# Token-major projections with 512 weight columns in one pass instead of 256 in each of two

## The chip, the cores and the metric

The kernel runs on one core of a Trainium2 chip. The metric is the device time of one execution, in microseconds; the times before and after are medians of several runs. Matmuls run on TensorE (PE in the profile, its weight loads PEld), elementwise work on VectorE (DVE) and ScalarE (ACT), transfers are issued from SyncE (SP) and GpSimd (POOL).

## The reference

Two layers of a hybrid block work on 512 latent tokens and 256 context tokens of 1024 features. In each layer the modulated, normalized tokens `h` are multiplied by one input matrix, whose columns feed three mixers and their gates:

```
glu, q, k, v, rq, rk, rv, rg, gates = split(h @ w_in[l] + b_in[l])
a   = conv_module(glu, ...)                       # depthwise convolution over 31 tokens
att = latent_attention(rope(rms(q)), rope(rms(k)), v, k_c, v_c)   # 8 query heads, 2 key heads
ret = bidir_retention(rq, rk, rv, ...)            # 8 heads, a mean and a norm taken per head
x   = x + g1 * ((sig(ga) * (a @ w_pa) + sig(gb) * (att @ w_pb) + sig(gc) * (ret @ w_pc)) @ w_out)
x   = x + g2 * conv_ffn(modulate(rms(x)))
```

The change concerns two groups of columns of `w_in`: the 512 of the attention queries `q` (columns 1024 to 1535) and the 512 of the retention values `rv` (columns 2816 to 3327). In the second layer the context tokens are needed for keys and values only, so the queries there are those of the 512 latent tokens.

## The kernel before, in words

Activations lie feature-major: one tile of 128 features by 768 tokens for each of the KC = 8 input chunks. Every float32 operand is split exactly into a high and a low float32r part (`hh`, `hl` for activations, `whi`, `wlo` for weights), and a product is three matmuls: high by high, low by high, high by low.

Most products are feature-major (`dense`): a 128x128 weight block is stationary, the tokens are the moving operand, 512 latent columns and, where wanted, 256 context columns. Keys and values (unit K), attention queries (units Q0 and Q1) and retention values (units R0 and R1) are token-major (`tm`, `tm_chunks`): the activations of 128 tokens are stationary and 256 weight columns are the moving operand. A token tile of `tm` takes 8 chunks x 3 = 24 matmuls into one PSUM bank; a unit takes 6 token tiles, or 4 for the queries of the second layer. In the first layer K and Q0 are made in `start`, before the list of units begins; in the second layer K is made at the end of the feed-forward of the first.

Weights stream through SBUF once (`Stream`), in tiles of 128 x 1024 (`SUB`), 140 per layer, in the order of use. SP loads a raw tile; ACT makes its high part (L107), DVE its low part (L108). There are four places for split tiles (`WB = 4`) and two for raw ones (`RAWB = 2`). A tile's place is reused for the tile four further on, after the last matmul that reads it. `tm` walks over all token tiles with the weights of a unit in hand, so `wcols` passes `held` to `Stream.next`, which keeps all tiles of the unit in place:

```
self.prepare(min(self.cur - held, self.cur if self.kept is None else self.kept) + WB)
```

A unit of 256 columns is 8 blocks of 256, which is two weight tiles.

Dense products have four PSUM banks (`ND = 4`). A token tile of R is read out by DVE: the bias is added (L792), and the mean of each head is taken and subtracted (L795 to L797). A token tile of Q is read out by one DVE addition (L1028); the norm, rotation and transposition of queries and keys (`qk_post`) follow as side work.

The units of a layer stand in `ORDER` (L43). Beside them run generators of side work: the rest of K, Q0 and Q1, the attention and then the retention (`mixers`, begun by A), the convolution (begun by C), and in the first layer a part of the modulation. After each token tile or dense product `tick(us)` gives every generator credit, and it writes down as many of its steps as the credit buys. `mixers` first has K and Q0 finished. This gives the written order of the program. A planner then orders each engine's instructions by modelled times; among those that are ready, what is written earlier goes first. The engines run their queues in that order.

Of the kernel before, what the change touches and what calls it, by code (L numbers as in the profile page):

```python
"""Hybrid conv / GQA / retention DiT backbone on one core.

Activations are feature-major: a [128, T] tile per 128 features, with the latent tokens in
columns 0..511 and the context tokens in columns 512..767. Dense products run on the tensor
engine in float32r: every float32 operand is split exactly into two float32r parts and three
products of parts are accumulated. Weights stream through SBUF once, in the order of use.
"""
# [15 lines left out]
P = 128  # L23
# [10 lines left out]
SUB = 1024                      # columns of a weight tile  # L34
NSUB = 140                      # weight tiles of a layer
START = ((0, 256, 2), (256, 256, 0), (512, 256, 4), (768, 256, 0))  # columns of the first modulation, weight tiles after
ND = 4                          # PSUM banks of the dense products
RAWB, RAWA = 2, 2               # tiles of raw weights, of raw w_ada
WB = 4                          # split weight tiles
NSLOT = 47                      # activation tiles  # L40
# per layer: order of the units of the input projection (K keys and values, Q queries, R retention values,
# A attention and retention begin, G inputs of the convolution, C it begins, P retention heads, T gates)
ORDER = ('K Q0 R0 Q1 A R1 G0 C G1 G2 G3 P0 P1 P2 P3 T T T T',  # L43
         'K Q0 Q1 R0 A G0 C R1 G1 G2 G3 P0 P1 P2 P3 T T T T T T')
ATT_LEAD, RET_LEAD = (3, 2), (1, 1)   # head pairs by which the mixers may lag behind the projection
ATTR, RETR, CONVR, ADAR = (1.0, 1.0), (1.4, 1.6), (0.4, 0.4), (0.06, 0.2, 0.25)  # rates of the side work
QLAG = 2                        # query tiles between rotation and transposition
HOLDO, HOLDD = (4, 4), (4, 6)   # chunks of w_out, w_down done token part by token part
LEADO, LEADB = 2, ((0, 0, 0), (4, 0, 4))  # chunks of w_out, of the branches that start side by side
FIRST = (1, 2)                  # chunks of w_up done token part by token part  # L50
RSPLIT = (2, 3)                 # retention outputs split before the last is there
EARLY = 6                       # chunks of the merged branches split before the last is there
FILL = 5                        # input chunk after which the next token part's norm begins
PEP, DVP, LATE = (4,), (2, 3), (5,)   # vectors of the first modulation on PE, on DVE, on DVE in the FFN
# [12 lines left out]
def parts(segs):  # L67
    """the tokens in two parts"""
    if len(segs) > 1:
        return [[s] for s in segs]  # L70
    n = segs[0][1] // 2
    return [[(0, n)], [(n, n)]]


class Stream:
    """Weight tiles in order of use; the wanted blocks are recorded and laid out by the host."""
# [12 lines left out]
    def issue(self, upto):  # L89
        while self.issued < min(upto, self.limit):  # L90
            i = self.issued
            # tile RAWB takes a place of w_ada, which needs none of its own yet
            pool, tag = (self.k.apool, "rawa") if i == RAWB else (self.k.raw_pool, "raw")
            t = pool.tile([P, SUB], F32, tag=tag, name=f"raw{i}")
            self.k.nc.sync.dma_start(t, self.dram[i])
            self.raw[i] = t
            self.issued += 1
# [15 lines left out]
    def keep(self, cols):  # L113
        """holds the tiles from that of the next block on"""
        self.kept = self.cur + (self.off + cols > SUB)

    def release(self, tile=None):
        """lets go of the tiles before this one, or of all"""
        self.kept = tile
        self.prepare((self.cur if tile is None else tile) + WB)  # L120

# [40 lines left out]
class Kern:  # L162
# [26 lines left out]
    def dps(self):  # L189
        """a bank for a dense product"""  # L190
# [9 lines left out]
    def after(self, *ins):  # L200
        """What is traced inside is issued after these instructions on their engines."""
# [6 lines left out]
    def in_order(self):  # L208
        """What is traced inside keeps its order on the engines that compute."""
# [30 lines left out]
    def chunk(self, pts, w, x, k, n):  # L240
        """adds the products of input chunk k of n with a weight block"""
# [5 lines left out]
    def dense(self, key, xs, segs, ws=None):  # L247
        """key(k) names the 128x128 weight block that meets input chunk k; ws has them if they are kept."""
# [7 lines left out]
    def last_chunks(self, key, xs, segs, hold, evac, norm, lead=0):  # L256
        """The products for all output chunks, the first ones (lead) side by side, the last ones (hold)
        token part after token part, with the norm of a part under the products of the next; returns
        the norm of the last part."""
# [36 lines left out]
    def pair(self, banks, ws, xs, segs, mid=None):  # L296
        """two products side by side, input chunk after input chunk, for some tokens"""
# [9 lines left out]
    def group(self, keys, xs, segs):  # L307
        """several products side by side, input chunk after input chunk"""
# [67 lines left out]
    def ada_load(self, l, pc, c0, w, slots=False):  # L376
        """columns c0 .. c0 + w of vector pc of w_ada, row blocks side by side, in tiles"""
# [12 lines left out]
    def ada_part(self, l, pc, c0, w, raws=None):  # L390
        """columns c0 .. c0 + w of vector pc of the modulation"""
# [30 lines left out]
    def coefs(self, l, pc, a, n, nv):  # L422
        """the factors that chunks a .. a + n of vector pc give, for the first nv of c and c_ctx"""
# [17 lines left out]
    def ada_rows(self, l, pieces):  # L441
        """vectors of the modulation of layer l on the vector engine: each row of the transposed w_ada
        times c and, where it is used, times c_ctx, summed"""
# [38 lines left out]
    def rstd2(self, pts, name, y=None):  # L482
        """-2 * rsqrt(v + eps) for the PSUM pieces of v."""
# [11 lines left out]
    def sq_add(self, m, x, segs, last=False):  # L495
        """adds the squares of chunk m; those of the last chunk may be kept apart"""
# [24 lines left out]
    def norm(self, l, which, xs, out):  # L521
        """how to normalize and modulate some tokens of xs for layer l, into tiles that are put in out"""
# [36 lines left out]
    def gate_from(self, pts, m):  # L559
        """tanh(z / 2) = 2 * sigmoid(z) - 1 of a projected chunk"""  # L560
# [5 lines left out]
    def gated(self, th, pts, m, T):  # L566
        """2 * sigmoid * (a projected chunk and its bias)"""
# [121 lines left out]
    def decay(self, h):  # L689
        """wa[:, c], c < 768, and wb[:, 640 + c - 768]: decay of latent or context tokens among  # L690
        themselves at c = query - 128 * key tile + 384; wb[:, c], c < 640: decay of context keys for
        latent queries at c = query - 128 * key tile + 128."""
# [95 lines left out]
    def rv_unit(self, u):  # L788
        nc = self.nc
        for tt, pt in self.tm(self.wcols(2816 + 256 * u), 6):  # L790
            d = self.rv[tt][:, 256 * u:256 * u + 256]
            nc.vector.tensor_tensor(d, pt, self.brow2[:, 256 * u:256 * u + 256], op=ALU.add)  # L792
            d3 = d.rearrange("p (h d) -> p h d", h=4)
            m = self.sm(4, "rvm")
            nc.vector.tensor_reduce(m, d3, axis=AX.X, op=ALU.add)  # L795
            nc.vector.tensor_scalar(m, m, 1.0 / 64, None, op0=ALU.mult)
            nc.vector.tensor_tensor(d3, d3, m.rearrange("p (h o) -> p h o", o=1).to_broadcast([P, 4, 64]),  # L797
                                    op=ALU.subtract)

    def tm(self, wb, nt):  # L800
        """token-major product of 256 columns: the activations are the stationary operand."""
        for tt in range(nt):
            pt = self.dps()
            ts = slice(tt * P, tt * P + P)
            for k in range(KC):
                xh, xl = self.h[k]
                wh, wl = wb[k]
                for i, (x, w) in enumerate(((xh, wh), (xl, wh), (xh, wl))):
                    self.mm(pt[:, :256], x[:, ts], w, k == 0 and i == 0, k == KC - 1 and i == 2)
            yield tt, pt[:, :256]  # L810
            self.tick(2.65)

    def tm_chunks(self, wb, tiles, mid=None):
        """the token-major product of 256 columns for some token tiles, input chunk after input chunk"""
# [14 lines left out]
    def start(self):  # L829
        """First layer: norm, modulation, keys and the first queries by input chunks as they come;  # L830
        returns the products for kv_unit and q_unit."""
# [17 lines left out]
    def first_products(self, xs, ada):  # L849
# [4 lines left out]
        def go(stage, c0):  # L854
            """stage 0: products of the modulation, 1: to columns, 2: the rest"""
# [71 lines left out]
    def wcols(self, c0):  # L927
        return [self.W.next(("w_in", self.l, k * P, c0), 256, k // 4) for k in range(KC)]
# [19 lines left out]
    def qk_post(self, raw, nh, t0, nt, tab, dst, scale=None, rs=None):  # L948
        """raw [128 tokens, nt, nh*64] (with bias) -> roped, transposed with a copy on each partition
        half, and handed to dst(tile, PSUM [128, nh*128]); scaled by the reciprocal root mean square  # L950
        and scale, or without scale and the reciprocal root mean square left in rs [128, nt*nh]."""
# [70 lines left out]

# [571 lines left out]
```

## Time and profile before

| | |
|---|---|
| runs | 2387.57, 2387.9, 2388.31 us; median 2387.9 us |
| profiled execution, first to last instruction (span) | 2385.8 us |
| time of that execution around its span | not shown by the page; the median of the runs is 2.1 us above the span |
| PE busy | 2347.9 us, 98%, 13426 matmuls |
| PE weight loads busy | 1941.3 us, 81% |
| DVE busy | 1566.2 us, 66% |
| ACT busy | 896.0 us, 38% |
| granted TensorE clock, mean | 0.998 |

An engine's busy time is the time in which at least one of its instructions is on record. Matmuls overlap one another in the pipeline, so the duration of one matmul is longer than the distance from its start to the next start; a sum of durations is more than the engine's time. Where a row tells an idle time, it is that of the engine just before the instructions of the row, with what ended it.

### The profile page before, as it was taken

To read this page: it belongs to the slowest core of one execution; us is meant where nothing else is said; L and a number is where in the kernel's file an instruction comes from. 1 tells how busy PE (TensorE), PEld (TensorE's weight loads), DVE (VectorE), ACT (ScalarE), POOL (GpSimd) and SP (SyncE) were. 2 spreads that over 40 slices of the span, in tenths; PEclk is the share of its full clock that TensorE was granted. 3 is DMA by queue.
4 is the path that set the end of the run, shared out by engine and by line. 5 is a ranking of instruction groups with operands and counts; after the bars stand their busy time and mean duration, and the time that the engine had idled before them with its cause. 6 is when DMAs were issued, how large, how long until landed. Compare 5 with 4: busy or idle time off the path is not lost.

```text
span 2385.8 us, 33890 instructions
## 1 busy us (share of the span) xinstructions
PE 2347.9 (98%) x13426; PEld 1941.3 (81%) x13426; DVE 1566.2 (66%) x3174; ACT 896.0 (38%) x1505; POOL 62.6 (3%) x122
## 2 busy tenths in 40 slices
PE   6999999999999999999999999999999999999998
PEld 5988876678888888888888889887558889888887
DVE  6887858688874476645763359878688546544445
ACT  3465644422232342213122234565443433423233
POOL 0000010000000000000000000001100000000000
PEclk9999999999999999999999999999999999999999
DMA  7221122213343123323661121113223322332322
GB/s 287 96 65 60 63 80 69 71 62 115 107 142 105 54 73 118 118 97 101 210 210 62 62 98 54 55 61 102 70 67 112 131 98 80 106 97 97 97 97 71
DMA packets 69119, 234.13 MB, mean 98 GB/s; under 512 B 8640, under 2 KB 10960, under 8 KB 68960
## 3 DMA queue, kind: packets, MB, share of 16 engines
q1 hardware_dynamic: 59616, 203.64, 25.8%
q0 software_dynamic: 9344, 28.32, 4.1%
q8 instruction: 106, 1.74, 0.3%
q14 instruction: 53, 0.43, 0.1%
HBM read 213.57 MB, written 6.82 MB: 92 GB/s over the span
## 4 chain that ended last, share of the span: by engine, by line
PE 95%; DVE 3%; issue 1%; DMA 1%; ACT 0%; SPq 0%; DVEq 0%; ACTq 0%
PE pd L197 81%; PE ps L197 12%; PE ps L1090 2%; DVE ht L543 0%; DVE wlo L108 0%; PE ps L1003 0%; DVE hl L555 0%; DMA x<-xt 0%; DVE qq L1038 0%; DMA raw<-wstream 0%; ACT whi L107 0%; DVE sq L508 0%; DVE mod L418 0%; DVE rstdt L491 0%; DVE rstd L492 0%
## 5 line engine op out<-in xcount | busy, mean ns | idle before, releaser
L197 PE MATMUL pd<-hl,whi 128*128 128x512 f32 (+1 forms) x2176 | 658.6, 354 | 1.9 <-DVE hl L555 1.7
L197 PE MATMUL pd<-hh,wlo 128*128 128x512 f32 (+1 forms) x2176 | 659.9, 355 | 0.0
L197 PE MATMUL pd<-hh,whi 128*128 128x512 f32 (+1 forms) x2176 | 656.9, 354 | 1.4 <-DVE fy L1387 0.9
L107 ACT ACTIVATE whi<-raw 128x1024 fp32r<-128x1024 f32 x280 | 296.7, 1061 | 930.9 <-PE pd L197 840.6
L108 DVE TENSOR_TENSOR wlo<-raw,whi 128x1024 fp32r<-128x1024 f32 x280 | 341.6, 1221 | 261.8 <-ACT whi L107 258.7
L197 PEld LDWEIGHTS pd<-hh,whi 128*128 128x128 f32 x2176 | 361.9, 188 | 69.5 <-issue 8.3
L197 PEld LDWEIGHTS pd<-hl,whi 128*128 128x128 f32 x2176 | 360.3, 188 | 68.9 <-issue 8.3
L197 PEld LDWEIGHTS pd<-hh,wlo 128*128 128x128 f32 x2176 | 360.8, 188 | 64.6 <-issue 9.4
L608 DVE SCALAR_TENSOR_TENSOR cacc<-u,vec,cacc 128x497 f32<-128x497 f32 (+9 forms) x360 | 221.4, 648 | 1.9
L197 PE MATMUL pd<-hidh,wlo 128*128 128x512 f32 (+1 forms) x558 | 169.1, 348 | 0.0
L197 PE MATMUL pd<-hidh,whi 128*128 128x512 f32 (+1 forms) x558 | 167.9, 346 | 0.0
L197 PE MATMUL pd<-hidl,whi 128*128 128x512 f32 (+1 forms) x558 | 167.3, 345 | 0.0
L1073 ACT ACTIVATE prob<-ps,amx,qrs 128x256 f32<-128x256 f32 (+1 forms) x144 | 93.7, 656 | 90.8 <-DVE amx L1068 77.5
L197 PE MATMUL pd<-whi,hl 128*128 128x256 f32 x416 | 120.1, 289 | 3.9 <-DVE hl L555 3.9
L197 PE MATMUL pd<-whi,hh 128*128 128x256 f32 x416 | 120.5, 292 | 2.8 <-ACT hh L552 2.8
L197 PE MATMUL pd<-wlo,hh 128*128 128x256 f32 x416 | 119.3, 287 | 0.0
L1430 DVE SCALAR_TENSOR_TENSOR x<-pd,mod,x 128x512 f32<-128x512 f32 (+1 forms) x102 | 62.1, 632 | 81.0 <-PE pd L197 80.7
L466 DVE SCALAR_TENSOR_TENSOR rowa<-rowa,crow 128x768 f32<-128x768 f32 (+1 forms) x144 | 94.2, 686 | 26.2 <-DMA rowa<-wadt 26.2
L197 PEld LDWEIGHTS pd<-hidh,whi 128*128 128x128 f32 x558 | 94.9, 189 | 14.9 <-issue 0.2
L1395 DVE TENSOR_TENSOR fy<-fy,pd 128x512 f32<-128x512 f32 x66 | 37.5, 596 | 104.2 <-PE pd L197 101.4
L197 PEld LDWEIGHTS pd<-hidl,whi 128*128 128x128 f32 x558 | 93.7, 188 | 14.1 <-issue 0.2
L197 PEld LDWEIGHTS pd<-hidh,wlo 128*128 128x128 f32 x558 | 94.3, 189 | 13.0
(236 smaller groups left out, 3251.4 us busy)
## 6 DMA issues: line engine op xcount, KB each, us to landing
raw<-wstream SPq DMA_DIRECT2D x280, 512.0 KB, 3.5
rowa<-wadt SPq DMA_DIRECT2D x72, 512.0 KB, 4.1
adar<-wada SPq DMA_DIRECT2D x16, 384.0 KB, 7.6
stk<-rkh POOLq DMA_DIRECT2D x32, 192.0 KB, 4.9
rawa<-wada SPq DMA_DIRECT2D x8, 512.0 KB, 3.6
x<-xt SPq DMA_DIRECT2D x8, 384.0 KB, 7.6
x<-xt POOLq DMA_DIRECT2D x8, 384.0 KB, 4.4
adar<-wada SPq DMA_DIRECT2D x8, 256.0 KB, 7.5
```

Of the source, the lines that this page charges most:

```text
L107: nc.scalar.activation(hi, r, AF.Copy)
L108: nc.vector.tensor_tensor(lo, r, hi.bitcast(F32), op=ALU.subtract)
L197: return self.nc.tensor.matmul(out, w, x, start=start, stop=stop)
L466: nc.vector.scalar_tensor_tensor(out, raw[:, a:b], 1.0, t[:, o:o + b - a], op0=ALU.mult, op1=ALU.mult, accum_out=acc[:, c, j, h:h + 1])
L608: nc.vector.scalar_tensor_tensor(acc[:, a:b], u[:, a + d:b + d], w(k), acc[:, a:b], op0=ALU.mult, op1=ALU.add)
L1073: nc.scalar.activation(pr[:, o - k0:o - k0 + c], pt[:, :c], AF.Exp, scale=rs, bias=mx[:, 2:3], accum_out=sm[:, j:j + 1])
L1090: nc.tensor.transpose(pt[:, b * P:b * P + P], pr[:, o + b * P:o + b * P + P], self.ident)
L1395: nc.vector.tensor_tensor(y[:, o:o + n], y[:, o:o + n], pt, op=ALU.mult)
L1430: nc.vector.scalar_tensor_tensor(xs[m][:, s], pt, g2[:, m, j:j + 1], xs[m][:, s], op0=ALU.mult, op1=ALU.add)
```

## The change

Retention values are made by one pass `R` with 512 weight columns in both layers, in place of R0 and R1. In the second layer the queries are made by one pass `Q` with 512 columns, in place of Q0 and Q1; the first layer keeps Q0 (in `start`) and Q1. In the first layer the pass R comes after A, where R1 was, and Q1 comes directly after K and Q0. In the second layer A comes after Q, and R where R1 was, after G0 and C. A unit of 512 columns is 8 blocks of 512, four weight tiles, and all of them are held. Each token tile fills one PSUM bank with 512 columns, and both halves are read out by the same DVE instructions as before. The credit of a token tile with 512 columns is twice that with 256. Comments are taken out in the rest of the diff.

```
-ORDER = ('K Q0 R0 Q1 A R1 G0 C G1 G2 G3 P0 P1 P2 P3 T T T T',
-         'K Q0 Q1 R0 A G0 C R1 G1 G2 G3 P0 P1 P2 P3 T T T T T T')
+ORDER = ('K Q0 Q1 A R G0 C G1 G2 G3 P0 P1 P2 P3 T T T T',
+         'K Q A G0 C R G1 G2 G3 P0 P1 P2 P3 T T T T T T')
...
-    def rv_unit(self, u):
+    def rv_unit(self):
         nc = self.nc
-        for tt, pt in self.tm(self.wcols(2816 + 256 * u), 6):
-            d = self.rv[tt][:, 256 * u:256 * u + 256]
+        for tt, pt in self.tm(self.wcols(2816, 512), 6, 512):
+            for u in range(2):
+                d = self.rv[tt][:, 256 * u:256 * u + 256]
+                c = slice(256 * u, 256 * u + 256)
+                nc.vector.tensor_tensor(d, pt[:, c], self.brow2[:, c], op=ALU.add)
...
-    def tm(self, wb, nt):
+    def tm(self, wb, nt, cols=256):
...
-                    self.mm(pt[:, :256], x[:, ts], w, k == 0 and i == 0, k == KC - 1 and i == 2)
-            yield tt, pt[:, :256]
-            self.tick(2.65)
+                    self.mm(pt[:, :cols], x[:, ts], w, k == 0 and i == 0, k == KC - 1 and i == 2)
+            yield tt, pt[:, :cols]
+            self.tick(2.65 * cols / 256)
...
-    def wcols(self, c0):
-        return [self.W.next(("w_in", self.l, k * P, c0), 256, k // 4) for k in range(KC)]
+    def wcols(self, c0, cols=256):
+        return [self.W.next(("w_in", self.l, k * P, c0), cols, k * cols // SUB) for k in range(KC)]
...
+    def q_units(self, nt):
+        raws = [], []
+        for tt, pt in self.tm(self.wcols(1024, 512), nt, 512):
+            for u in range(2):
+                self.q_raw(u, tt, pt[:, 256 * u:256 * u + 256], raws[u])
+        return [self.q_post(u, nt, raws[u]) for u in range(2)]
...
+            elif step == "Q":
+                qk["Q0"], qk["Q1"] = (self.side(g) for g in self.q_units(nt))
...
             elif kind == "R":
-                self.rv_unit(i)
+                self.rv_unit()
```

`q_raw` is the addition of the bias that stood in `q_unit`, and `q_post` the rest of `q_unit`.

## Rows read from the trace of the kernel before

**Rows 1.** The page: busy share by engine, and the chain that ended last.
```profile
PE 2347.9 (98%) x13426; PEld 1941.3 (81%) x13426; DVE 1566.2 (66%) x3174; ACT 896.0 (38%) x1505; POOL 62.6 (3%) x122
...
PE 95%; DVE 3%; issue 1%; DMA 1%; ACT 0%; SPq 0%; DVEq 0%; ACTq 0%
```

**Rows 2.** Waits of PE, longest first: total us, times, longest us.
```profile
PE ps L197 <- DVE sq L508: 14.7, 1, 14.7
PE pd L197 <- DVE hl L555: 5.6, 6, 2.2
```

**Rows 3.** Busy us of PE, PEld, DVE, ACT, POOL, then clock, by stretch.
```profile
77.00:95.00 18.00, 18.00 (x140) 16.06 (x139) 15.62 (x60) 5.98 (x15) 0.00 (x0) 1.00 0.33 118
95.00:111.00 16.00, 16.00 (x130) 14.57 (x129) 14.97 (x48) 8.19 (x24) 0.00 (x0) 1.00 0.18 57
...
1508.00:1541.00 33.00, 32.98 (x290) 30.60 (x290) 26.77 (x74) 18.84 (x49) 0.00 (x0) 1.00 0.05 18
```

**Rows 4.** Groups of matmuls by shape: busy us, mean ns of one.
```profile
L197 PE MATMUL pd<-hh,whi 128*128 128x512 f32 x1376 | 544.6, 396 | 0.9 <-DVE fy L1387 0.9
...
L197 PE MATMUL pd<-whi,hh 128*128 128x256 f32 x416 | 120.5, 292 | 2.8 <-ACT hh L552 2.8
```

**Rows 5.** The chain from 70 to 150 us: start, us, piece, matmuls in it.
```profile
74.41 2.88 PE pd L197 x24
```

**Rows 6.** The chain from 1780 to 1900 us, feature-major products of 512 tokens.
```profile
1791.55 47.42 PE pd L197 x209
```

**Rows 7.** Timeline of PE, end of R1 in the second layer: start, us.
```profile
1536.29 1.53 PE L197 MATMUL ps<-probt,vt 128*64 128x128 f32 x24
...
1539.13 0.36 PE L197 MATMUL pd<-whi,hl 128*128 128x256 f32 x1
...
1540.40 0.28 PE L197 MATMUL pd<-wlo,hh 128*128 128x256 f32 x1
1540.52 0.40 PE L197 MATMUL pd<-hh,whi 128*128 128x512 f32 x1
...
1541.91 0.39 PE L197 MATMUL pd<-hh,whi 128*128 128x512 f32 x1
```

**Rows 8.** Timeline of ACT, then of DVE, at the end of R1, second layer.
```profile
1537.13 1.07 ACT L107 ACTIVATE whi<-raw 128x1024 fp32r<-128x1024 f32 x1
...
1542.75 1.22 DVE L108 TENSOR_TENSOR wlo<-raw,whi 128x1024 fp32r<-128x1024 f32 x1
```

**Rows 9.** Timeline of ACT, then of DVE, 93 to 111 us, first layer.
```profile
93.41 1.06 ACT L107 ACTIVATE whi<-raw 128x1024 fp32r<-128x1024 f32 x1 [1.44 <-issue]
...
107.28 1.22 DVE L108 TENSOR_TENSOR wlo<-raw,whi 128x1024 fp32r<-128x1024 f32 x1
...
109.26 1.23 DVE L108 TENSOR_TENSOR wlo<-raw,whi 128x1024 fp32r<-128x1024 f32 x1
110.51 0.42 DVE L1028 TENSOR_TENSOR qraw<-pd,brow 128x256 f32<-128x256 f32 x1
```

**Rows 10.** Single lines: min/median/max ns, first and last start in us.
```profile
L792 DVE TENSOR_TENSOR rv<-pd,brow x24: 408/418/426, 79.0 to 1541.4; 128x256 f32<-128x256 f32 x24
...
L1028 DVE TENSOR_TENSOR qraw<-pd,brow x16: 411/416/426, 74.5 to 1472.2; 128x256 f32<-128x256 f32 x16
...
L108 DVE TENSOR_TENSOR wlo<-raw,whi x280: 1182/1224/1229, 26.6 to 2352.8; 128x1024 fp32r<-128x1024 f32 x140
```

**Rows 11.** Lines L795 and L797, in the same columns.
```profile
L795 DVE TENSOR_REDUCE rvm<-rv x24: 377/412/421, 79.6 to 1542.4; 128x4 f32<-128x256 f32 x24
...
L797 DVE TENSOR_TENSOR rv<-rv,rvm x24: 407/416/426, 81.0 to 1546.8; 128x256 f32<-128x256 f32 x24
```

**Rows 12.** Timeline of PE in Q0 of the second layer.
```profile
1444.29 0.54 PE L197 MATMUL pd<-whi,hh 128*128 128x256 f32 x2
...
1445.98 0.28 PE L197 MATMUL pd<-whi,hl 128*128 128x256 f32 x1
```

**Rows 13.** The page's DMA issues: KB each, us from issue to landing.
```profile
raw<-wstream SPq DMA_DIRECT2D x280, 512.0 KB, 3.5
```

More of the change, by code (lines that the diff above doesn't have):

```diff
@@ L786, in ret_gen @@
         self.ret_out[p] = y
-    def rv_unit(self, u):
+    def rv_unit(self):
         nc = self.nc
-        for tt, pt in self.tm(self.wcols(2816 + 256 * u), 6):
-            d = self.rv[tt][:, 256 * u:256 * u + 256]
[L792 to L798, printed above, removed]
-    def tm(self, wb, nt):
+        for tt, pt in self.tm(self.wcols(2816, 512), 6, 512):
[3 more added lines that the diff above has]
+                nc.vector.tensor_tensor(d, pt[:, c], self.brow2[:, c], op=ALU.add)
+                d3 = d.rearrange("p (h d) -> p h d", h=4)
+                m = self.sm(4, "rvm")
+                nc.vector.tensor_reduce(m, d3, axis=AX.X, op=ALU.add)
+                nc.vector.tensor_scalar(m, m, 1.0 / 64, None, op0=ALU.mult)
+                nc.vector.tensor_tensor(d3, d3, m.rearrange("p (h o) -> p h o", o=1).to_broadcast([P, 4, 64]),
+                                        op=ALU.subtract)
+    def tm(self, wb, nt, cols=256):
         for tt in range(nt):
@@ L1021, in kv_unit, with q_raw, q_post @@
         return self.qk_post(kraw, 2, 0, 6, self.tabs[1], dst, 0.125)
-    def q_unit(self, u, nt, prods=None):
+    def q_raw(self, u, tt, pt, raws):
+        o = (tt % 3) * 256
+        if o == 0:
+            raws.append(self.S("qraw"))
+        self.nc.vector.tensor_tensor(raws[-1][:, o:o + 256], pt, self.brow1[:, 256 * u:256 * u + 256], op=ALU.add)
+    def q_unit(self, u, nt, prods=None):
+        raws = []
+        for tt, pt in prods or self.tm(self.wcols(1024 + 256 * u), nt):
+            self.q_raw(u, tt, pt, raws)
+        return self.q_post(u, nt, raws)
+    def q_units(self, nt):
[4 more added lines that the diff above has]
+        return [self.q_post(u, nt, raws[u]) for u in range(2)]
+    def q_post(self, u, nt, raws):
         nc = self.nc
-        raws = [self.S("qraw") for _ in range((nt + 2) // 3)]
-        for tt, pt in prods or self.tm(self.wcols(1024 + 256 * u), nt):
-            o = (tt % 3) * 256
-            nc.vector.tensor_tensor(raws[tt // 3][:, o:o + 256], pt, self.brow1[:, 256 * u:256 * u + 256], op=ALU.add)
         qq = self.qq[u] = [self.S("qq", F32R) for _ in range((4 * nt + 5) // 6)]
```

## The prediction

> **What bounds the kernel now.** I read the page first: PE is busy for 98% of the span, and 95% of the chain that ended last is PE work [rows 1]. A busy PE can still hide waits, so the waits of PE came next: the longest is a single one of 14.7 us, at the first norm, the second group has 5.6 us in six waits [rows 2]. The change touches neither. So each microsecond of matmul issue that goes is worth a microsecond, as long as no wait takes its place. The view by stretches says where that could happen: the clock is granted in full, PE is busy throughout, but DVE is busy for 15.62 of 18.00 us during R0 of the first layer, 14.97 of 16.00 us in most of Q1, and 26.77 of 33.00 us during R1 of the second layer [rows 3]. DVE is the second bound exactly where the change works.
>
> **The matmuls.** The grouped rows are a trap: a matmul of 256 columns is on record with 292 ns, one of 512 with 396 ns [rows 4], as if two small ones cost 188 ns more than a large one. These durations overlap. What counts is the distance between starts. R0's first token tile is 24 matmuls of 256 columns in 2.88 us, 120.0 ns each [rows 5]. Feature-major matmuls of 512 columns, undisturbed, take 47.42 us for 209, 226.9 ns each [rows 6]. One of 512 in place of two of 256 saves 240.0 - 226.9 = 13.1 ns. Beside the attention the 512-column matmul is a little slower: six of them start from 1540.52 to 1541.91 us, 231.7 ns each [rows 7], while 256 columns still take 120 ns there; that pair saves 8.3 ns.
>
> How many pairs: a token tile has 24 matmuls. R0 and R1 with 6 tiles each are 144 pairs in each layer, Q0 and Q1 of the second layer with 4 tiles are 96. So 768 matmuls become 384. The 288 pairs of R now lie behind A, beside attention: 288 x 8.3 ns = 2.39 us. The 96 of Q lie before A: 96 x 13.1 ns = 1.26 us. Sum 3.65 us. No row shows a matmul with stationary activations and 512 moving columns; the rows on both sides bound it by 384 x 8.3 = 3.2 us and 384 x 13.1 = 5.0 us, and by nothing at all if the small fixed part should not be saved there.
>
> The Trainium skill speaks against even this: by "TensorE: Matmul & The Clock Gate", section "Back-to-back issue gap", an isolated matmul at full clock takes its columns at 2.4 GHz plus 2.5 ns. By that a pair would save 2.5 ns, 384 pairs 1.0 us. The trace does not agree: 120.0 and 226.9 ns are each some 13 ns above their columns at that clock, so the rows decide.
>
> **The read-out.** DVE does the same instructions on the same shapes: per half of a token tile of R an addition of 418 ns [rows 10], a reduction of 412 ns and a subtraction of 416 ns [rows 11], 1.25 us, and 0.42 us per half of Q [rows 10]. I cost this at nothing. A bank is now held until both halves are read, but a token tile takes 24 x 0.227 = 5.4 us instead of 2.9, so four banks cover a DVE that is up to 16 us behind instead of 9; if that cover were gone, a tile would cost PE its 2.5 us of read-out.
>
> **The weights.** This is where the change can lose. A unit of 512 columns holds four weight tiles, and there are only four places. Before, the next unit's two tiles were split while a unit ran. Now the first place comes free when the last token tile has used its first two chunks (6 of 24 matmuls), and the next unit can start 18 matmuls later, 18 x 0.227 = 4.1 us. In that time ACT must make the high part (1.06 us [rows 9]) and DVE the low part (1.22 us [rows 10]): 2.28 us if both are free. Behind a late split nothing on DVE needs it, but on PE the next product stands in the queue, and all later work with it.
>
> How late is it really? At the end of R1 in the second layer the high part starts at 1537.13 us and the low part ends at 1542.75 + 1.22 = 1543.97 us [rows 8]: 6.8 us, since DVE first does what was written before. The place came free just before the attention block that starts at 1536.29 us, so it is 7.7 us in all. PE's cover after the change would be 18 matmuls at 231.7 ns, 4.2 us, and the attention block that stands inside this token tile, 1536.29 to 1539.13 us [rows 7], 2.8 us: together 7.0 us. That leaves a wait of 0.7 us; without an attention block at that place 3.5 us; with a free DVE none. I take 0.7 us for this end of R, half, 0.4 us, for that of the first layer, where no convolution has been written yet, and 0 for the end of Q, which lies before the attention, so that 2.28 us fit into 4.1. Each has 0 and 3.5 us as its ends.
>
> The start of R needs the split, too: two of its tiles are ready, the other two wait for the places of the unit before. In the first layer this is worst. Before, two low parts came at 107.28 and 109.26 us although ACT was ready with the first at 94.5 us: DVE kept them behind 13 us of earlier-written work, and the read-out of Q1, written later, came after them, at 110.51 us [rows 9]. That work goes down by the six read-outs of R0 (6 x 1.25 = 7.5 us) and up by those of Q1 (6 x 0.42 = 2.5 us), so the two low parts would end near 103.5 and 105.5 us. Q1, in the place of R0, ends near 95 us; the first token tile of R has 12 matmuls of cover, 2.7 us, and would wait 6.4 us in all. But the planner doesn't keep to the written order of token tiles: in Q0 of the second layer two first matmuls of a triple stand one behind the other at 1444.29 us, and a second one without its first comes at 1445.98 us [rows 12]. So it can put the first 12 matmuls of three further token tiles, 3 x 2.7 = 8.2 us, ahead of the wait. I take 0 there and in the second layer, with 6.4 us as the upper end. The tiles after these four are no issue: the raw ones land 3.5 us after their issue [rows 13], and a feature-major chunk uses up one tile in 5.4 us or more.
>
> **What moves.** The attention begins one pass earlier in both layers, with as much side work per microsecond of dense work. It has no PE work of its own to lose, since dense matmuls stand beside it at all times; its DVE work comes into the stretch where R's read-outs are. I cost that at nothing, covered by the idle 19% of DVE in the second layer's R1 [rows 3]; if DVE falls behind by more, it shows as the late splits above. SP issues the same 280 weight loads in another order; POOL's transfers are untouched.
>
> **Sum.** -3.65 + 0.7 + 0.4 = -2.55 us on the profiled execution's span of 2385.8 us, 2383.25 us. That execution's time around the span isn't shown; I leave the 2.1 us between span and median in place: 2387.9 - 2.55, about 2385.4 us.
>
> **Rivals.** (1) Late weight splits decide. The planner keeps token tiles in order, PE waits 6.4 us at the start of R in the first layer, and 3.5 us at both ends of R: 13.4 - 3.65 = +9.8 us, 2397.7 us. For it speak the 13 us that a low part lay behind other work, against it that no wait of PE in these stretches is among its two longest groups [rows 2], and the order within Q0 [rows 12]. It turns the sign from 3.7 us of waits on, and it is a measurable loss from 8.4 us on.
> (2) The full price of 13.1 ns applies to all 384 pairs and nothing new is waited for: -5.0 us, 2382.9 us. For it speaks that R's stretch before the attention's first scores is undisturbed; against it the 231.7 ns beside attention.
> (3) The fixed part of a matmul isn't saved when the activations are stationary; nothing is gained and the waits of 1.1 us stay: 2389.0 us. Against it: the same 13 ns stand above the columns in both kinds of matmul. The skill's page that was named would put the time between this and the forecast.
>
> **How the numbers follow.** A measurement of this kernel can tell about 0.2%, 4.8 us, from no change. My forecast, a small gain mostly below that, has 0.43; its own range is 2383 to 2388 us. Rival 1 has 0.23, rival 2 0.27, rival 3 0.07. The forecast and rival 3 are no measurable change: 0.50. Rival 2 lies just past the lower edge, 2383.1 us: faster 0.27. Rival 1 is slower: 0.23. The range goes from 2382.0, rival 2 with a microsecond of waits that vanish elsewhere, to 2394.0 us, which takes in rival 1 with half of its waits and leaves out its worst.
>
> **What would show it.** In the profile after, PE should have 13042 matmuls, 384 fewer; 24 matmuls of R before the attention should take about 5.44 us, beside it 5.56 us. If these come out near 5.76 us, rival 3 is right. At the ends and starts of R, the waits of PE for L108 and L107 should stay below 2 us in all; a wait of several microseconds there is rival 1, and the forecast is wrong. If the order of the first R shows no interleaved token tiles and yet no wait, my account of DVE's backlog is wrong. DVE's busy time should stay near 1566 us.

## The result, and the profile after

The changed kernel takes 2416.47 us (2414.89 to 2420.26), the kernel before 2387.96 us (2387.57 to 2388.31) beside it: a ratio of 1.0121, 95% interval 1.0109 to 1.0134, slower by 28.5 us. The forecast was 2385.4 us, range 2382.0 to 2394.0. The profiled execution, with 2420.26 us the slowest of the four, has a span of 2418.5 us, 32.7 us above that of before.

The page of the changed kernel: busy time by engine, and the chain that ended last.

```profile
PE 2355.0 (97%) x13042; PEld 1925.2 (80%) x13042; DVE 1567.1 (65%) x3174; ACT 902.5 (37%) x1509; POOL 62.8 (3%) x122
...
PE 92%; DVE 5%; ACT 2%; issue 1%; DMA 1%; SPq 0%; DVEq 0%; ACTq 0%
```

Against [rows 1], 384 matmuls are gone, and still PE's part of the chain has fallen from 95% to 92%, and ACT has come in with 2%. The waits of PE say where (total us, times, longest us):

```profile
PE ps L197 <- DVE sq L508: 14.7, 1, 14.7
PE ps L197 <- ACT prob L1091: 14.3, 9, 3.0
PE pd L197 <- DVE hl L555: 6.8, 7, 2.2
PE ps L1108 <- ACT prob L1091: 4.6, 4, 1.6
...
PE ps L1005 <- ACT prob L1091: 1.6, 1, 1.6
PE ps L1108 <- DVE asm L1094: 1.3, 1, 1.3
PE ps L197 <- ACT probt L1109: 1.1, 1, 1.1
...
PE pd L197 <- DVE rv L794: 0.9, 1, 0.9
...
PE pd L197 <- ACT whi L107: 0.3, 1, 0.3
```

The groups of [rows 2] are nearly as they were. New are those with prob, probt and asm, the tiles of attention's softmax: attention's matmuls (and, for 1.6 us, a transposition of queries, L1005) wait for them. 14.3 + 4.6 + 1.6 + 1.3 + 1.1 = 22.9 us. Such a wait only shows when PE has nothing else to run. Busy us of PE, PEld, DVE, ACT, POOL and the granted clock in the worst such stretch, first the changed kernel, then the kernel before:

```profile
152.00:166.00 14.00, 9.37 (x50) 6.92 (x48) 10.42 (x47) 7.29 (x21) 0.54 (x1) 0.63 0.16 48
```
```profile
152.00:166.00 14.00, 14.00 (x106) 11.57 (x106) 9.10 (x29) 8.51 (x20) 0.54 (x1) 1.00 0.40 124
```

PE runs 50 matmuls there instead of 106, at a mean granted clock of 0.63. The timeline of PE in the changed kernel shows what is missing (start, us, names; in brackets the idle time and its releaser):

```profile
152.03 0.40 PE L197 MATMUL pd<-hh,wlo 128*128 128x512 f32 x1
154.04 0.98 PE L1108 MATMUL ps<-cst,prob 128*128 128x128 f32 x6 [1.62 <-ACT prob L1091]
156.18 0.79 PE L197 MATMUL ps<-kh,qq 128*128 128x512 f32 x1 [1.15 <-ACT probt L1109]
...
159.73 0.69 PE L1108 MATMUL ps<-cst,prob 128*128 128x128 f32 x2 [1.05 <-ACT prob L1091]
160.35 2.83 PE L197 MATMUL ps<-probt,vt 128*64 128x128 f32 x24
...
166.06 0.39 PE L197 MATMUL pd<-hh,whi 128*128 128x256 f32 x1 [0.88 <-DVE rv L794]
```

A dense matmul (pd) starts at 152.03 us, the next at 166.06 us, released by a read-out of R. Between them stands attention alone, each piece waiting for the softmax of its own. After the first idle stretches the granted clock falls to its lower level, 1.2 GHz, from 155.3 us for 10.2 us: the 24 matmuls of probt take 2.83 us where they took 1.53 at 2.4 GHz [rows 7]. That stretch in the columns used above:

```profile
155.30:165.50 10.20, 7.96 (x42) 6.30 (x42) 7.56 (x38) 4.61 (x14) 0.00 (x0) 0.50 0.09 34
```

The read-out that ends the time without dense work, in the timeline of DVE, and before it, in that of PE, the last matmul of the product that is read:

```profile
126.14 0.39 PE L197 MATMUL pd<-wlo,hh 128*128 128x512 f32 x1
```
```profile
164.90 0.17 DVE L684 TENSOR_SCALAR lgt<-lgt 128x16 f32<-128x16 f32 x1
165.11 0.17 DVE L685 TENSOR_TENSOR lgt<-lgt,lgs 128x16 f32<-128x16 f32 x1
165.20 0.42 DVE L794 TENSOR_TENSOR rv<-pd,brow 128x256 f32<-128x256 f32 x1
165.53 0.15 DVE L1097 RECIPROCAL asm<-asm 128x1 f32<-128x1 f32 x1
165.60 0.40 DVE L794 TENSOR_TENSOR rv<-pd,brow 128x256 f32<-128x256 f32 x1
```

This is R's fourth token tile, as the order of the program's instructions tells: 39 us lay between product and read-out, and DVE was not the reason, being idle for 3.6 of the 14 us above. Where the time went: compared with the trace of before, dense work falls behind by 13.0 us between the end of Q0 and the FFN of the first layer, and by 18.7 us between the start of K in the second layer and the end. Together that is 31.7 of the 32.7 us; the start and the FFN are within about 1 us of before.

### The profile page after: what moved, and what is told of

Same layout as the page of the kernel before. It is cut to its first block, busy times and chain, and to the rows that moved or that the text cites. A ratio compares the mean times of both kernels' runs of the same rounds, so it can differ in the third digit from the quotient of the medians.

```text
span 2418.5 us, 33130 instructions
## 1 busy us (share of the span) xinstructions
PE 2355.0 (97%) x13042; PEld 1925.2 (80%) x13042; DVE 1567.1 (65%) x3174; ACT 902.5 (37%) x1509; POOL 62.8 (3%) x122
## 4 chain that ended last, share of the span: by engine, by line
PE 92%; DVE 5%; ACT 2%; issue 1%; DMA 1%; SPq 0%; DVEq 0%; ACTq 0%
PE pd L197 78%; PE ps L197 12%; PE ps L1108 2%; ACT prob L1091 1%; DVE wlo L108 1%; DVE amx L1084 1%; DVE ht L543 0%; ACT whi L107 0%; DMA raw<-wstream 0%; PE ps L1005 0%; DVE hl L555 0%; DVE cacc L608 0%; DMA x<-xt 0%; DVE qq L1056 0%; DVE sq L508 0%
## 5 line engine op out<-in xcount | busy, mean ns | idle before, releaser
L197 PE MATMUL pd<-whi,hl 128*128 128x256 f32 (+1 forms) x288 | 97.3, 339 | 5.1 <-DVE hl L555 5.1
L197 PE MATMUL pd<-whi,hh 128*128 128x256 f32 (+1 forms) x288 | 97.4, 342 | 2.1 <-ACT hh L552 2.1
L197 PE MATMUL pd<-wlo,hh 128*128 128x256 f32 (+1 forms) x288 | 96.7, 338 | 0.0
```

The lines of the kernel that those rows point to most:

```text
L197: return self.nc.tensor.matmul(out, w, x, start=start, stop=stop)
```

## The experiments

Two quantities appear in all of them. *Share of a layer*: by how much a layer's dense work fell behind (+) or ran ahead (-) of the trace of before, over the two stretches just named, from one profiled run each. Programs that have a layer in common show how well it repeats: the first layer of five runs gave -4.5, -4.4, -3.9, -2.8 and -2.4 us, the second layer of three -2.2, -1.4 and +1.4. The second share takes in the layer boundary near 1421 us, where the lower clock lasts differently long from run to run: in mid3, mid35 and mix3 2.2 to 2.3 us of it arise in the dense work that the kernel before does between 1420 and 1440 us. *Lead*: at each score matmul of attention, the dense work that PE has already done although it is written behind that score, less what is written ahead of it and not done, at 226.9 and 120.0 ns per matmul of 512 and 256 columns [rows 6, 5]. It is worked out from PE's records and the written order of the program. It answers how far the projection has run away from attention. The highest lead orders the runs only roughly: 22 us go with shares of -1.5, +9.5, +10.6 and +12.6. The first scores are counted from the start of the run, so that in the second layer they contain what the first layer lost or gained.

| run | what is written | first score, us | lead at it / highest, layer 1 | layer 2 | share 1 | share 2 | ratio, 95% interval |
|---|---|---|---|---|---|---|---|
| before | | 122, 1498 | 2 / 13 | 0 / 10 | 0 | 0 | 1 |
| after | | 117, 1509 | 9 / 26 | 17 / 24 | +13.0 | +18.7 | 1.0121 (1.0109 to 1.0134) |
| claim | after, R's tiles begun early | 117, 1502 | 9 / 25 | 18 / 35 | +5.8 | +20.1 | 1.0112 (1.0098 to 1.0125) |
| order256 | after's order, 256 columns | 107, 1497 | 3 / 15 | 7 / 14 | +11.4 | +10.6 | 1.0095 (1.0081 to 1.0109) |
| r512_early | R first, attention late | 159, 1539 | 7 / 17 | 0 / 16 | +25.2 | +9.5 | 1.0147 (1.0133 to 1.0160) |
| q512 | before, one pass Q in layer 2 | 122, 1498 | 2 / 13 | 0 / 14 | -1.0 | -1.1 | 0.9992 (0.9983 to 1.0001) |
| mid3 | attention from R's 4th tile | 130, 1497 | 5 / 17 | 3 / 19 | -4.5 | +9.0 | 1.0019 (1.0010 to 1.0028) |
| r512_beforeA | attention after R | 149, 1515 | 0 / 15 | 0 / 16 | +0.5 | +10.2 | 1.0042 (1.0029 to 1.0055) |
| order256_mid | 256 columns, attention after R0 | 133, 1495 | 7 / 12 | 0 / 10 | -1.1 | +4.9 | 1.0022 (1.0013 to 1.0031) |
| pace | after, slower attention | 117, 1509 | 9 / 22 | 17 / 22 | +12.6 | +10.6 | 1.0094 (1.0081 to 1.0107) |
| mix3 | layer 1 of mid3, layer 2 of q512 | 130, 1496 | 5 / 17 | 0 / 14 | -4.4 | +1.4 | 0.9989 (0.9980 to 0.9998) |
| mix2 | layer 1 from R's 3rd tile | 126, 1497 | 6 / 22 | 0 / 14 | -1.5 | -1.4 | 0.9999 (0.9990 to 1.0008) |
| mix4 | layer 1 from R's 5th tile | 132, 1496 | 0 / 12 | 0 / 14 | -2.1 | -2.2 | 0.9995 (0.9986 to 1.0004) |
| g0first | layer 2: G0 before R | 132, 1498 | 5 / 17 | 4 / 22 | -2.8 | +9.5 | 1.0039 (1.0026 to 1.0051) |
| mid3_pace2 | mid3, slower in layer 2 | 130, 1496 | 5 / 17 | 3 / 14 | -3.9 | +4.2 | 1.0002 (0.9993 to 1.0010) |
| mid35 | mid3, from the 6th tile in layer 2 | 132, 1508 | 5 / 17 | 0 / 12 | -2.4 | +4.5 | 1.0002 (0.9993 to 1.0010) |

**First round: late read-outs, held weights, order, or the wide pass?** The trace suggested the late read-outs. In the program they have a reason: of the tiles that share the pool of 47 buffers, all 1188 are begun (written for the first time) in written order, in both kernels, so a read-out that begins a tile of R's results stands behind every attention step that was written before it (each begins a tile prob). Free tiles were not short: 6 to 12 of the 47 lay free in the order of the instructions where the late tiles were begun.

*claim* begins R's four tiles early.

```diff
         self.rv = [_Rv(self.rvt, t) for t in range(6)]
+        for t in self.rvt:
+            nc.vector.memset(t[:, 0:1], 0.0)
```

> The changed kernel, plus four one-column writes that begin the four tiles of the retention values at the start of the layer, ahead of attention; nothing else differs. Theory 1 (late read-outs): in the changed kernel R's read-outs stand behind attention's steps in VectorE's order (17 score maxima precede the read-out of the fourth token tile where 5 scores had begun at its end; in the second layer 94 against 80), and until they run R's token tiles keep all four banks of dense products; with the tiles begun early the read-outs stand right behind their token tiles, so PE's waits for ACT prob L1091 and for DVE rv vanish and the time is 2382 to 2392 us. Theory 2 (four held weight tiles make the splits late): nothing changes, 2412 to 2420. Theory 3 (attention that begins one pass earlier is by itself slower): 2405 to 2418. Theory 4 (a 512-column token-major product is slower than two of 256 beside attention): 2410 to 2420.

Measured 2414.49 us: theory 1 had said 2382 to 2392 and fell. The read-outs did come early: R's last one starts at 142 us in the first layer instead of 176, and at 1535 us in the second instead of 1590; the second is the end of this row, of the line of R's addition in claim:

```profile
L794 DVE TENSOR_TENSOR rv<-pd,brow x24: 404/417/425, 109.4 to 1535.2; 128x256 f32<-128x256 f32 x24
```

The first layer took back 7.2 of its 13.0 us, the second lost as much as before, later. Windows of claim and then of the kernel before, in the columns used above:

```profile
152.00:166.00 14.00, 13.73 (x104) 11.92 (x103) 12.62 (x52) 8.81 (x24) 0.00 (x0) 1.00 0.45 129
1574.00:1606.00 32.00, 20.17 (x141) 15.57 (x140) 20.17 (x50) 17.02 (x47) 0.54 (x1) 0.84 0.08 25
```
```profile
1574.00:1606.00 32.00, 32.00 (x237) 25.87 (x236) 20.31 (x52) 20.72 (x52) 0.54 (x1) 1.00 0.17 57
```

The hole at 152 us is gone and one of 32 us has opened at 1574 us; from its timeline:

```profile
1574.22 0.39 PE L197 MATMUL pd<-hh,wlo 128*128 128x512 f32 x1
1576.29 0.50 PE L197 MATMUL ps<-kh,qq 128*128 128x512 f32 x1 [1.68 <-ACT prob L1091]
...
1586.11 0.71 PE L197 MATMUL ps<-kh,qq 128*128 128x512 f32 x1 [2.91 <-ACT prob L1091]
...
1604.73 0.51 PE L197 MATMUL ps<-kh,qq 128*128 128x512 f32 x1 [1.06 <-ACT prob L1091]
```

The same picture, attention alone on PE, but no longer because of R. The read-outs were the gate at which the projection was stopped; with that one open it ran further ahead (lead up to 35 us) to the next, the read-outs of G, whose tiles are begun in written order too. The last matmuls of three of G's products start at 1554, 1564 and 1574 us, and ACT reads them at 1617, 1627 and 1635 us. In ACT's timeline, the read-out just before dense work goes on at 1606.61 us, and the next:

```profile
1605.86 0.70 ACT L563 ACTIVATE sg<-pd,hbin 128x512 f32<-128x512 f32 x1
...
1616.98 0.68 ACT L571 ACTIVATE u<-pd,vec 128x512 f32<-128x512 f32 x1
```

*order256* has the order of the changed kernel with the old passes.

```diff
-ORDER = ('K Q0 R0 Q1 A R1 G0 C ...',
-         'K Q0 Q1 R0 A G0 C R1 G1 ...')
+ORDER = ('K Q0 Q1 A R0 R1 G0 C ...',
+         'K Q0 Q1 A G0 C R0 R1 G1 ...')
```

> The kernel before with its 256-column units, in the order of the changed kernel: K Q0 Q1 A R0 R1 in the first layer, K Q0 Q1 A G0 C R0 R1 in the second. Theory 1: R0's read-outs now begin their tiles behind attention too (in VectorE's order 12 to 17 maxima against 3 to 6 scores begun, 94 to 100 against 83 to 96), so it is slower than before by 10 to 35 us: 2398 to 2423. Theory 2: two weight tiles are held as before, 2386 to 2390. Theory 3: as slow as the changed kernel or more, 2410 to 2420. Theory 4: 2386 to 2390.

Measured 2410.39 us, 0.95% slower without one matmul of 512 columns in its token-major products. Theories 2 and 4 are out as the main cause: most of the loss comes with the order. Its lead reaches only 15 us; four banks hold less here, 4 x 2.88 = 11.5 us of R [rows 5].

*r512_early* has the wide pass in R0's old place.

```diff
-ORDER = ('K Q0 Q1 A R G0 C ...',
-         'K Q A G0 C R G1 ...')
+ORDER = ('K Q0 R Q1 A G0 C ...',
+         'K Q R A G0 C G1 ...')
```

> The changed kernel with its one pass R put ahead of attention: K Q0 R Q1 A in the first layer, K Q R A G0 C in the second; same units, same four held weight tiles. Theory 1: no attention step is written before the read-outs, so none stands before them: 2381 to 2387 (before less the 3.65 us of matmuls, plus what attention loses by starting half a pass later). Theory 2: the splits are as late as in the changed kernel or later, 2395 to 2420. Theory 3: 2383 to 2392, by the later start of attention alone. Theory 4: 2386 to 2400.

Measured 2423.07 us, above the ranges of all four. Theory 2's, 2395 to 2420, is nearest, but PE's waits for low parts come to 1.4 us in all; its longest new wait is another:

```profile
PE pd L197 <- ACT u L571: 9.3, 2, 5.6
```

The first score comes 36 and 41 us later than before, 25 of the 41 brought along from the first layer, and with it all that follows: in the first layer attention's matmuls end at 357 us instead of 325, retention's at 524 instead of 498. Lateness alone is not shown to cost the 25 us: *r512_beforeA* below has its first score at 149 us and loses 0.5 us in that layer. The trace shows the stop at G's read-outs again: a product of G whose last matmul starts at 175 us is read at 206 us here; in *r512_beforeA* the first two, at 163 us, are read at 169 us. Why the gap is so much wider here was not tried.

*q512* is the kernel before with the one pass for the second layer's queries alone.

```diff
-         'K Q0 Q1 R0 A G0 C R1 G1 ...')
+         'K Q R0 A G0 C R1 G1 ...')
```

> The kernel before with one edit: the queries of the second layer in one pass of 512 columns (96 pairs fewer), R0 and R1 as before. Theory 1: 2386 to 2388.5, that is 1.3 us for the matmuls less than before, or nothing of it. Theory 2: four weight tiles held at Q, 2388 to 2396. Theory 4: 2390 to 2400. Theory 3 says nothing of it.

Measured 2386.08 us, ratio 0.9992 (0.9983 to 1.0001), with a share of -1.1 us where 1.26 were worked out. Its first layer, which was not changed, has -1.0 us too, so the matmul gain is not shown by it. It holds four weight tiles at Q and loses nothing that can be told: theory 2 is out for Q, and the next round takes it up for R.

**Second round: the lead.** Theory 5 took shape: steps of attention are written beside dense work by its estimated time. Work that PE does between the end of the queries and the first score counts as attention's company although attention can't run yet. In the changed kernel that is R from its first token tile on. PE runs ahead, its four banks (4 x 5.46 = 21.8 us of R) fill up, and since tiles are begun in written order the read-outs wait for attention to catch up.

*mid3* writes attention in from R's fourth token tile on.

```diff
+            if tt == at:
+                go()              # mix = self.side(mixers())
...
-ORDER = ('K Q0 Q1 A R G0 C ...',
-         'K Q A G0 C R G1 ...')
+ORDER = ('K Q0 Q1 R3 G0 C ...',   # R3: at = 3
+         'K Q R3 G0 C G1 ...')
```

> The changed kernel with attention written in from the fourth token tile of the one R pass on, in both layers (first K Q0 Q1, then R with attention from its fourth tile, then G0; second K Q, R with attention from its fourth tile, then G0 C). Lead means the dense work that PE has done although it is written after the attention step that PE begins: 0 to 13 us in the kernel before, 15 to 26 in the changed one, up to 32 with the early tiles. Theory 5 (lead): steps of attention are written beside dense work that PE does before the first score can begin; tiles of a pool are begun in written order, so dense work is stopped by its four banks once the lead is used up, and PE has attention alone. With 16.4 us of R written ahead of attention the lead at the first score is 0 to 9 us, and the time 2383 to 2394 us. Theory 3 (only the time of the first score counts, each us that it is later costs one): the first score comes 3 to 15 us later than before in each layer, 2394 to 2410.

Measured 2391.02 us, 25 us less than the changed kernel with the same passes, held weights and matmuls. The lead at the first score is 5 and 3 us. In its page and its waits the softmax has all but gone:

```profile
PE 2347.1 (98%) x13042; PEld 1918.7 (80%) x13042; DVE 1565.8 (66%) x3174; ACT 893.0 (37%) x1503; POOL 63.2 (3%) x122
```
```profile
PE ps L197 <- DVE sq L508: 14.6, 1, 14.6
PE pd L197 <- DVE hl L555: 5.8, 7, 1.4
PE pd L197 <- ACT hh L552: 2.4, 2, 1.9
PE ps L197 <- ACT prob L1093: 2.2, 2, 2.0
```

The first layer gains 4.5 us, the second still loses 9.0. Theory 3 is refuted in its plain form: the first score is 8 us later than before in the first layer, and the layer is faster.

*r512_beforeA* writes attention behind the whole of R, `K Q0 Q1 R A G0` and `K Q R A G0`.

> The changed kernel with the whole R pass ahead of attention and after both passes of queries: K Q0 Q1 R A in the first layer, K Q R A G0 C in the second (the second as in the run r512_early, the first with Q1 ahead of R). Theory 5: no lead to speak of, but attention is written a whole pass later and its last steps find less dense work: the first layer loses 3 to 15 us, the second as much as in r512_early (about 12): 2395 to 2415. Theory 3: the first score comes 10 to 20 us later than before in the first layer and 41 in the second: 2405 to 2425.

Measured 2397.07 us, as theory 5 had it; in the first layer +0.5 us, less than the 3 to 15 expected. With *after* (0 token tiles ahead of attention), *mix2* (2), *mid3* (3) and *mix4* (4) the first layer makes a series: +13.0, -1.5, -4.5 to -2.4, -2.1, +0.5 us for 0, 2, 3, 4 and 6 token tiles. The best places lie inside the pass; between 2, 3 and 4 single profiled runs can't decide.

*order256_mid* is its counterpart in 256 columns, `K Q0 Q1 R0 A R1 G0` in both layers.

> The kernel before, 256-column passes, with attention written in between R0 and R1 in both layers (K Q0 Q1 R0 A R1 G0 C). Theory 5: the same amount of R ahead of attention as in the run mid3, so within 4 us of it after the 3.65 us of matmuls are taken off: 2385 to 2396. Theory 3: 2390 to 2400. That the 512-column unit itself costs something beside attention (theory 4): 10 us or more faster than mid3.

Measured 2392.25 us, 1.2 us above mid3: the place of attention decides, not the width (theory 4 out). Its second layer loses 4.9 us although its lead goes no higher than in the kernel before (10), so part of the second layer's loss has another cause. In that layer its order differs from the kernel before in one thing: R1 stands ahead of G0 and C.

*pace* leaves the changed kernel's order and writes attention more thinly.

```diff
-ATTR, RETR, ... = (1.0, 1.0), (1.4, 1.6), ...
+ATTR, RETR, ... = (0.75, 0.75), (1.4, 1.6), ...
```

> The changed kernel with attention's steps written at three quarters of the rate, so that one step stands beside 5.9 us of dense work instead of 4.4. Theory 5: the lead is worked off faster, below 15 us in the second layer where it was 15 to 22, and PE's waits for ACT prob L1091 shrink by half or more: 2398 to 2412. Theory 3: first score as in the changed kernel, attention and retention end later: 2416 to 2430.

Measured 2410.95 us, just inside theory 5's 2398 to 2412. The two largest waits for prob go from 14.3 and 4.6 to 2.1 and 4.3 us, and in the second layer the lead, 17 at the first score, is below 13 from 1580 us on, where that of the changed kernel never falls below 13.6, with a share of +10.6 instead of +18.7 us. In the first layer nothing is won: the hole comes before the slower pace can tell.

**Third round: a version that keeps the gain.** All four have mid3's kind of first layer; *mix2*, *mix3* and *mix4* have q512's second layer.

```diff
+ORDER = ('K Q0 Q1 R3 G0 C ...',             # mix2: R2, mix4: R4
+         'K Q H0 A G0 C H1 G1 ...')         # H0, H1: the old R0, R1 in 256 columns
...
+         'K Q G0 C R1 G1 ...')              # g0first: one R, attention from its second tile
```

> First layer as in the run mid3 (one R pass, attention written in from its fourth token tile), second layer as in the run q512 (queries in one pass, R0, attention, G0, C, R1 in 256 columns). In mid3 the first layer's share of the work ends 6.2 us earlier than in the kernel before and in q512 the second layer's gives 1.1 us; theory 5 expects the two to add up, since each layer has its own lead: 2377 to 2382 us. Rival (the gain of the first layer is only shifted, and the second layer's start takes it back): 2384 to 2388.

> As mix3, with attention written in from the third token tile of R in the first layer: 5.5 us less dense work ahead of it. Theory 5: the lead at the first score and beside attention is about 5 us higher than in mix3 and reaches 20 us, the bound of four banks of 5.5 us, for a part of the layer: 1 to 8 us slower than mix3. Rival (the place does not matter as long as it lies inside R): within 1 us of mix3.

> As mix3, with attention written in from the fifth token tile of R in the first layer: 5.5 us more dense work ahead of it. Theory 5: the lead is about 5 us lower than in mix3, no stop at the banks, attention up to 5 us later: between 1 us faster and 4 us slower than mix3. Rival: within 1 us.

*mix3* measures 2383.78 us, 1.8 us above theory 5's range; with a ratio of 0.9989 (0.9980 to 0.9998) it is still the one version that is below the kernel before by its interval, if narrowly, and one of fourteen that were tried. Its second layer has +1.4 us where the same program in mix2 and mix4 has -1.4 and -2.2, so that nothing says the gain is taken back there. *mix2*, 2387.13 us, is 3.4 us slower than mix3, with a lead up to 22 us, as expected; *mix4*, 2384.80 us, cannot be told from mix3.

> First layer as in mix3; second layer K Q G0 C R with attention from R's second token tile: 11 us of G0 and 5.5 us of R ahead of attention, as much as the 17 us of R0 in the kernel before, and the one R pass of 512 columns kept. Theory 5: the second layer loses nothing of the kernel before, or up to 5 us since products of four banks of 5.5 us let the lead grow further: 2377 to 2386. Rival (a 512-column R beside attention in the second layer costs by itself, 9 us in mid3): 2387 to 2392.

*g0first* measures 2394.62 us, outside theory 5's 2377 to 2386 and above the rival's 2387 to 2392: as much dense work ahead of attention as in the kernel before did not do. Its lead still climbs to 22 us, though, and PE's longest new wait is the old one:

```profile
PE ps L197 <- ACT prob L1105: 7.0, 5, 1.9
```

I take it that what the work ahead must amount to was wrong, not what happens when it is too little. Left open was whether the second layer's 9 us are the lead or the wide pass.

**Fourth round: the second layer.** *mid3_pace2* is mid3 with `ATTR = (1.0, 0.75)`, *mid35* is mid3 with `R5` in place of `R3` in the second layer.

> The run mid3 with attention's steps in the second layer written at three quarters of the rate, 5.9 us of dense work beside one step instead of 4.4; the first layer as in mid3. In mid3 the first layer gains 4.5 us and the second loses 9.0, with a lead of 10 to 17 us there. Theory 5: the lead in the second layer falls below 10 us from its middle on and the loss of the second layer goes down by 3 to 9 us, unless attention ends so much later that retention pays: 2382 to 2389 us. Rival (a 512-column R in the second layer costs by itself, whatever the lead): 2390 to 2396.

> The run mid3 with attention of the second layer written in from the sixth token tile of R instead of the fourth, 10.9 us more dense work ahead of it. Theory 5: the lead in the second layer is 5 to 10 us lower than in mid3, but attention's first score is up to 8 us later and its last steps have less dense work: 2385 to 2394. Rival (512-column R by itself): 2390 to 2394, with the second layer's loss where it was, near 1600 us.

2387.92 and 2387.78 us, both 1.0002 (0.9993 to 1.0010): the whole change, both layers in wide passes, without a loss. The highest lead in the second layer goes from 19 to 14 and 12 us, the share from +9.0 to +4.2 and +4.5 (in mid35 although the first score comes some 12 us later than in mid3, 4 of them from the first layer). Without the 2.3 us at the layer boundary in mid3 and mid35 it goes from 6.7 to 4.2 and 2.2, so that the lower time of both runs says more than the shares. The rival that the wide pass costs by itself fell. What remains, 2 to 5 us, is about the amount that order256_mid loses there with 256 columns (+4.9); common to the three is that all of R stands ahead of G0 and of the start of the convolution. In order256_mid nothing else was changed in that layer, though it is one profiled run; for the wide pass this cause was not tried.

## Why the prediction was wrong

- **The matmuls** were right, and rather too cautious. 13042 are left. In the chain of the changed kernel, 24 of R's matmuls ahead of attention (from its first two token tiles, which stand interleaved), and 18 beside it:

```profile
106.64 5.46 PE pd L197 x24
...
1551.76 4.10 PE pd L197 x18
```

  227.5 and 227.8 ns each, so a token tile takes 5.46 and 5.47 us where 5.44 and 5.56 were forecast; rival 3's 5.76 is out. The wide matmul beside attention is as quick as ahead of it, so the 8.3 ns per pair were too low and 13.1 ns a little high: 240.0 - 227.5 = 12.5 ns, for 384 pairs 4.8 us. The Trainium skill ("TensorE: Matmul & The Clock Gate", "Back-to-back issue gap") has 512 / 2.4 GHz + 2.5 ns = 215.8 ns for an isolated matmul; the trace has 12 ns more here as well.
- **The read-out** was costed at nothing because "four banks cover a DVE that is up to 16 us behind instead of 9". That counted how fast DVE is. The read-out was 39 us behind by its place in the order, and that place follows from what was written before it, not from DVE's load. The trace of before had the sign of it: R1's fourth token tile in the first layer has its last matmul at 131.4 us and is read at 148.1 us. Nothing was made of it.
- **What moves** is the step that failed: "The attention begins one pass earlier in both layers ... It has no PE work of its own to lose, since dense matmuls stand beside it at all times". They do so only as far as they may be ahead of it. Written one pass earlier, attention began 5 us earlier in the first layer, at 117 us, and, with the 14 us by which the second layer itself started late taken off, 3 us earlier in the second, at 1509; its steps were written beside work that was over by then. The term was not nothing but +31.7 us (13.0 + 18.7), with the matmul gain already taken off. 22.9 us are seen as waits of PE for the softmax. PE's whole idle time, the span less its busy time, rose by 25.6 us. Beside attention the lower clock was granted in four stretches of 20.4 us in all, where the kernel before has none; PE was busy for 18.2 us of them, and at the ratio of 2.83 to 1.53 us, 8.3 of these are owed to the lower clock, an estimate. 25.6 + 8.3 us less the 4.8 us of matmuls is 29.1 of the 32.7 us by which the span grew; the rest is open.
- **The weights**: 0.7 + 0.4 us were forecast, PE waited 0.3 us for a high part and for no low part. Rival 1 did not come about, and q512, mid3 and its relatives, all with four held tiles, confirm it. The order within the first token tiles held the start of R free, as I took it: R's first two token tiles stand interleaved on PE between 101 and 112 us. [rows 12] showed the last product of K and the first token tile of Q0 interleaved, not two of Q0, and carries the reading all the same.
- **DVE** is busy for 1567.1 us, near 1566 as forecast. That an engine has room says nothing on when an instruction in its queue has its turn.
- The slower side had 0.23, all of it on rival 1. No rival held the mechanism that came: the loss of cover by an order that is written, not timed.

## What to carry to other kernels

When side work is interleaved by estimated time, ask of every moved unit not only what stands beside the side work, but whether the side work can already run when its company does: company spent before the first step can start is missing later, and the main work is then stopped by its banks. Where buffers are handed out in written order, a read-out waits for all that was written before it, however free its engine is; freeing one such gate here only moved the stop to the next. A wider unit that saves matmuls also takes a seam out of the schedule, and the seam may be worth several times the matmuls: keep it by starting the side work in the middle of the unit.

## What the runs showed of the hardware

- A matmul with stationary activations and 512 moving columns costs 227.5 ns from start to start, so one in place of two of 256, at 120.0 ns each [rows 5], saves 12.5 ns.
- A stretch in which PE waits for 1 to 2 us at a time costs twice: in 152 to 166 us, PE busy for 9.37 of 14.00 us, the granted clock was 0.63 on the mean, and what PE did there ran at 1.2 GHz for 10.2 us; with claim's 13.73 of 14.00 us it stayed at 1.00.
- At the layer boundary near 1421 us the lower clock lasted 6.8 us in mix3's profiled run and 3.4 us in those of mix2 and mix4, with the same second layer behind it: this is where most of the 3 us arises by which their shares differ. In mid3 and mid35 it lasted 6.8 us too, in the kernel before and in mid3_pace2 3.4 us.
